# Hybrid attention block: softmax shares taken on the probabilities in place, next query's transposes moved, gate sums and last output block regrouped

## The chip, the cores and the metric

One core of a Trainium2 chip runs the whole program. The time is device microseconds of one execution. The kernel before was timed in three runs; the profile is of a further, single execution. Engines are named as in the profile: PE (TensorE, products), PEld (its weight loads), DVE (VectorE), ACT (ScalarE), POOL (GpSimd), SP (SyncE, which issues nearly all transfers).

## The reference

One layer of a diffusion backbone over 512 latent tokens and 256 context tokens, width 2048, float32. Both streams are normalised and modulated, and projected by one matrix `w_in`. Eight heads of a gated DeltaNet and eight heads of grouped-query attention follow; their gated outputs are concatenated and projected by `w_out`, and the residual sum is normalised:

```python
def attend(q_blk, k_all, v_all):
    s = jnp.einsum('bqkgd,bskd->bkgqs', q_blk, k_all).astype(jnp.float32) * (HEAD_DIM ** -0.5)
    p = jax.nn.softmax(s, axis=-1).astype(v_all.dtype)
    return jnp.einsum('bkgqs,bskd->bqkgd', p, v_all)

attn_lat = block_attention(qa, k_all, v_all) * jax.nn.silu(z_a)
y = jnp.concatenate([gdn_lat, attn_lat], axis=-1) @ w_out
x = x + gate * y                 # gate = (silu(c) @ w_ada + b_ada), last third
return rms_norm(x, final_norm_w)
```

Queries are 512 latent tokens by 8 heads of 128; keys and values are 768 tokens by 2 heads.

## The kernel before, in words

Large products are taken as three float32r products (`mm3`, L145 to L148): high by high, high by low and low by high part, where the high part is a cast on ACT and the low part a subtraction on DVE. Transposes and a few small products stay float32.

The program runs in stages: modulation and first projections (to 160 us), DeltaNet heads with the remaining projections as filler (to 876 us), attention with gate projections as filler (876 to 1114 us), the output projection in four column blocks of 512 (to 1293 us), and the last normalisation and store.

**Attention** is a loop over 17 steps, written at the end of the program's listing below. Step `u` works on half a head, 256 queries (a unit). On PE a unit has, in this order: transposes of the previous unit's probabilities (`pt`, two of three groups), the scores of this unit (`s`, 12 products), the third `pt` group, the spread of the previous unit's reciprocals (`ov`), filler steps, the values of the previous unit (`o`, 18 products of 256 columns), one filler step, the transposes of a query (`qtp`), two filler steps. A head's second unit transposes the next head's rotated query (`qn`) into `qTh` and `qTl`; a head's first unit transposes the raw query of the next head back to tokens for its norm.

PE, ACT, DVE and POOL run this stage in the order in which the code emits it; SP's order is set by a scheduler. So a DVE instruction that waits holds all behind it.

On ACT and DVE a unit has: the high and low parts of the transposed probabilities (`pth`, `ptl`), the row maximum of the scores (`mx`, L1260), two exponentials (`pr`, L1270) that also give the row sums, in second units the rotation of the next query (L1238 to L1241), two gate rows, filler work, two more gate rows, the result, the high and low parts of the next query. `attn_over` (L1275) then takes the reciprocals of the row sums and puts them on the diagonals of `dg`. One unit later `attn_spread` (L1296) multiplies ones by `dg` on PE, so that each reciprocal stands in a column for all partitions, and ACT copies the result to `ov`. `attn_values` (L1304) multiplies the values by `ov`; for ten units whose gate is there already it first multiplies the gate by `ov`.

PSUM buffers: `pt`, `ov` and `qtp` share two banks in turn (tag "t"); `s` has three, `o` one, filler `zl` two.

**Fillers.** `fillers` (L1344) projects 11 gate blocks (`zl`), 16 row tiles each in four weight pieces. A step is one row tile, three products. `z_piece` (L1338) loads a piece, two pieces ahead, and both casts it (`whi_z`) and subtracts (`wlo_z`). `z_over` closes a block: a Tanh on ACT, then `ze` and `M` on DVE. A unit runs FS, FV, FQ, FR = 4, 3, 1, 2 steps at the four places.

**Gate rows.** `gate_rows` (L1378) computes the output gate, a vector of 2048: 64 tiles of `w_ada` (`graw`) are multiplied by a column of `scol` and added into `gacc`, 16 tiles for each 512 columns. `gate_out` (L1369) sums `gacc` over partitions by a product with ones (`gater`), adds a row of `b_ada` and writes 512 values to memory (`grd`), four times in all. The rows are read back spread over all partitions (`gbc`) for the output stage.

**Last output block** (L1550 on): for each of four row tiles `t`, 48 products of 512 columns, `epilogue` (L1522: times gate, plus residual, square with row sum, times the norm's weights), the reciprocal root (`power`, on POOL), scaling of 2048 columns half on ACT and half on DVE, two transfers of 512 KB.

Of the kernel before, what the change touches and what calls it, by code (L numbers as in the profile page):

```python
# [8 lines left out]
F32 = mybir.dt.float32  # L9
F32R = mybir.dt.float32r  # L10
AF = mybir.ActivationFunctionType
# [57 lines left out]
def build(tc, a):  # L69
# [169 lines left out]
    def mul(eng, out, x, y):  # L239
        eng.tensor_tensor(out=out, in0=x, in1=y, op=ALU.mult)  # L240
# [970 lines left out]
    def ttile(shape, nm):  # L1211
        return PSt.tile(shape, F32, tag="t", bufs=2, name=nm)
# [3 lines left out]
    def attn_q(h):  # L1216
        qc = ap_.tile([128, SEQ], F32, tag="qc", bufs=2, name=f"qc{h}")
        SY.dma_start(qc, qad[h])
        return qc
# [52 lines left out]
            prs.append(pr)  # L1272
        return prs

    def attn_over(h, qp, mx):  # L1275

        dg = ap_.tile([128, 2, 128], F32, tag="dg", bufs=2, name=f"dg{h}_{qp}")
        V.reciprocal(mx[:, 1], mx[:, 1])
        V.tensor_tensor(out=dg, in0=ident.unsqueeze(1).to_broadcast([128, 2, 128]),
                        in1=mx[:, 1].unsqueeze(2).to_broadcast([128, 2, 128]), op=ALU.mult)  # L1280
        return dg

    def attn_pt(h, qp, prs, j2):

# [8 lines left out]
        split_from(tp3, pth, ptl)  # L1293
        return pth, ptl

    def attn_spread(h, qp, dg):  # L1296

        ov = ttile([128, 256], f"ov{h}_{qp}")
        T.matmul(ov, lhsT=ones, rhs=dg.rearrange("p a b -> p (a b)"), start=True, stop=True)
        over = ap_.tile([128, 256], F32, tag="ov", bufs=2, name=f"ov{h}_{qp}")  # L1300
        S.copy(over, ov)
        return over

    def attn_values(h, qp, pts, over):  # L1304
# [12 lines left out]

    done, early = set(), set()
# [19 lines left out]
    def z_piece(n):  # L1338
        i, kq = zs[n // 4], n % 4
        col = (COL_ZG if i < 8 else COL_ZA - 1024) + i * 128  # L1340
        src = w_in[kq * 512:(kq + 1) * 512, col:col + 128].rearrange("(k p) c -> p k c", p=128)
        return wpiece(src, f"z{i}_{kq}", 128, V)

    def fillers():  # L1344

        pieces = [z_piece(0), z_piece(1)]
        over = None
        yield
        for n in range(4 * len(zs)):
            i, kq = zs[n // 4], n % 4  # L1350
            if n + 2 < 4 * len(zs):
                pieces.append(z_piece(n + 2))
            if kq == 2 and outs:
                gate_out(*outs.pop(0))
            hi, lo = pieces.pop(0)
            if kq == 0:
                pl = PP.tile([128, SEQ], F32, tag="pl", name=f"zl{i}")
            for k4 in range(4):
                k = kq * 4 + k4
                for m, (lw, rt) in enumerate(((hi[:, k4], hhL[:, k]), (hi[:, k4], hl(0, k)), (lo[:, k4], hhL[:, k]))):  # L1360
                    T.matmul(pl, lhsT=lw, rhs=rt, start=k == 0 and m == 0, stop=k == KT - 1 and m == 2,  # L1361
                             skip_group_check=True)
# [6 lines left out]
    def gate_out(c, acc, row):  # L1369

        pr = PP.tile([128, 512], F32, tag="pl", name=f"gater{c}")
        T.matmul(pr[0:32], lhsT=ones[:, 0:32], rhs=acc, start=True, stop=True)
        V.tensor_tensor(out=row, in0=row, in1=pr[0:1], op=ALU.add)
        SY.dma_start(grd[:, c * 512:c * 512 + 512], row)

    outs = []

    def gate_rows():  # L1378

        def load(i):  # L1380
            c, k = divmod(i, KT)
            raw = ap_.tile([128, 512], F32, tag="graw", bufs=GB, name=f"graw{i}")
            SY.dma_start(raw, w_ada[k * 128:(k + 1) * 128, 2 * D + c * 512:2 * D + c * 512 + 512])
            return raw

        def bias(c):
            row = ap_.tile([128, 512], F32, tag="ze", bufs=2, name=f"grow{c}")[0:1]
            SY.dma_start(row, a["b_ada"][:, 2 * D + c * 512:2 * D + c * 512 + 512])
            return row

        raws = [load(i) for i in range(GB - 1)]
        acc = last = None
        yield
        for i in range(4 * KT):
            c, k = divmod(i, KT)
            raw = raws.pop(0)
            if k == 0:
                last, acc = acc, ap_.tile([128, 512], F32, tag="gacc", bufs=2, name=f"gacc{c}")
            if k == 0:
                V.tensor_scalar(out=acc, in0=raw, scalar1=scol[:, k:k + 1], scalar2=None, op0=ALU.mult)  # L1400
            else:
                V.scalar_tensor_tensor(out=acc, in0=raw, scalar=scol[:, k:k + 1], in1=acc, op0=ALU.mult, op1=ALU.add)  # L1402
            if i + GB - 1 < 4 * KT:
                raws.append(load(i + GB - 1))
            if k == 3 and c:
                outs.append((c - 1, last, bias(c - 1)))
            yield
        outs.append((3, acc, bias(3)))

    qcs = {i: attn_q(i) for i in (1, 2)}  # L1410
    for i in range(8):
# [21 lines left out]
    for u in range(2 * NH + 1):  # L1433
        h, qp = divmod(u, 2)
        more = h + 1 < NH
        prs, pts = None, []
        if before is not None:
            pts = [attn_pt(before[0], before[1], before[2], j2) for j2 in range(2)]
        if h < NH:
            sos, mx = attn_scores(h, qp, *qt, scs[h])  # L1440
        if before is not None:
            pts.append(attn_pt(before[0], before[1], before[2], 2))
            over = attn_spread(before[0], before[1], dg)
        if h < NH:
            prs = attn_exp(h, qp, sos, mx, scs[h])
            if qp == 1 and more:
                qn = next(qns)
            fill(FS + 5 * (before is None), 2)
        if before is not None:
            fill(FV, 2)  # L1450
            attn_values(before[0], before[1], pts, over)
        if u < NZA:

            e = ap_.tile([128, SEQ], F32, tag="ze", bufs=2, name=f"zae{u}")
            S.activation(e, M[8 + u], AF.Tanh, scale=0.5)
            silu(V, M[8 + u], M[8 + u], e)
            early.update(((u, 0), (u, 1)))
        fill(FQ)
        if more:
            if qp == 0:  # L1460
                qns = attn_norm(h + 1, qcs.pop(h + 1))
                next(qns)
                if h + 3 < NH:
                    qcs[h + 3] = attn_q(h + 3)
            else:
                qt = attn_qt(h + 1, qn)
        if h < NH:
            dg = attn_over(h, qp, mx)
        fill(FR)
        before = h, qp, prs  # L1470
    for _ in gen:
# [1 line left out]
    for _ in rows:  # L1473
        pass
    for o_ in outs:
        gate_out(*o_)
    es_m4.close()
    es_p0.close()
    es_p.close()
# [52 lines left out]
    for c in range(4):  # L1532
# [16 lines left out]
            wlast.append((hi, lo))  # L1549
        for t in range(4):  # L1550
            ts_ = slice(t * 128, t * 128 + 128)
            ps = PO.tile([128, 512], F32, tag="po", name=f"po3_{t}")
            for k in range(KT):
                mm3(ps, mh[k][:, ts_], ml[k][:, ts_], *wlast[k], k == 0, k == KT - 1)
            epilogue(c, t, ps)
            f = fr[:, t:t + 1]
            V.tensor_reduce(out=f, in_=fss[:, t], axis=AX.X, op=ALU.add)
            V.tensor_scalar(out=f, in0=f, scalar1=1.0 / D, scalar2=EPS, op0=ALU.mult, op1=ALU.add)
            power(f, -0.5)
            for q in range(2):  # L1560
                qs = slice(q * 1024, q * 1024 + 1024)
                if q == 0:
                    S.activation(yx[:, t, qs], yx[:, t, qs], AF.Copy, scale=f)
                else:
                    V.tensor_scalar(out=yx[:, t, qs], in0=yx[:, t, qs], scalar1=f, scalar2=None, op0=ALU.mult)
                SY.dma_start(a["out"][0, t * 128:t * 128 + 128, qs], yx[:, t, qs])
# [26 lines left out]
```

## Time and profile before

| what | value |
|---|---|
| median of 3 runs | 1307.14 us (1307.06 to 1307.84) |
| profiled execution, its own time | 1304.42 us |
| its span in the profile | 1302.6 us |
| PE, DVE, ACT, POOL busy | 1250.4, 842.5, 583.4, 141.9 us |
| attention, 876 to 1114 us | PE busy 232.84, DVE 187.25, ACT 116.52 of 238 us |
| output projection, 1114 to 1293 us | PE busy 178.9 of 179 us |
| after the last product, 1293 to 1302.6 us | PE 0, DVE 2.99, ACT 1.87 us |

In the profile a row of the timeline is: start, duration (both us, summed where `xN` merges instructions), engine, line, operation, tiles written and read, shape, and in brackets the idle time of the engine before it and what ended that. A line's name is that of the helper that emits it: L240 is the helper for a product of two tensors, L950 and L951 the split into high and low part, L1361 a filler's products. Matmul rows overlap, so the pace of PE is read from starts, not from durations.

### The profile page before, as it was taken

What the parts mean: (1) busy time and instruction counts of PE and PEld (TensorE: products, weight loads), DVE (VectorE), ACT (ScalarE), POOL (GpSimd) and SP (SyncE); (2) the same over time, 40 slices, a digit from 0 to 9 for tenths busy, and PEclk for the clock granted to TensorE, in tenths of its full rate; (3) what the DMA queues carried; (4) which work ended last, traced back from release to release, by engine and by line L of the source; (5) the groups of instructions that cost most, each with busy time, mean ns of one, the idle gap of its engine ahead of it and who ended that gap; (6) DMA issues with size and microseconds to landing.
All of it is one profiled execution on the core that took longest, in us unless ns stands there. A gap on an engine that the chain in (4) does not pass through costs nothing. (4 is left out here: it accounts for less than half of the span.)

```text
span 1302.6 us, 24348 instructions
## 1 busy us (share of the span) xinstructions
PE 1250.4 (96%) x9226; PEld 1018.4 (78%) x9226; DVE 842.5 (65%) x1893; ACT 583.4 (45%) x1464; POOL 141.9 (11%) x206
## 2 busy tenths in 40 slices
PE   6799999999999999999999999999999999999997
PEld 4466688888888888888888877787888888788885
DVE  5444596686867678675776646537888887555432
ACT  4222363455545454544545444535555444434211
POOL 1323100111111111111111001100000000000000
PEclk9999999999999999999999999999999999999998
DMA  9999424231332313222132443356443443475302
GB/s 354 316 326 347 133 67 107 60 67 55 74 72 62 78 47 83 67 69 57 54 83 75 106 131 110 99 164 214 149 129 114 123 140 102 161 244 190 93 33 97
DMA packets 227000, 164.53 MB, mean 126 GB/s; under 512 B 62210, under 2 KB 198491, under 8 KB 225859
## 3 DMA queue, kind: packets, MB, share of 16 engines
q1 hardware_dynamic: 226586, 162.87, 42.9%
q8 instruction: 73, 1.20, 0.4%
q14 instruction: 44, 0.36, 0.1%
q10 hardware_dynamic: 297, 0.11, 0.0%
HBM read 148.85 MB, written 14.08 MB: 125 GB/s over the span
## 5 line engine op out<-in xcount | busy, mean ns | idle before, releaser
L240 POOL TENSOR_TENSOR sdh<-sth,egl 128x256 f32<-128x256 f32 x80 | 56.9, 711 | 446.6 <-DVE sth L892 344.8
L871 ACT ACTIVATE oqh<-ksh,egsw 64x128 f32<-64x128 f32 x128 | 46.3, 362 | 92.7 <-DVE rh L866 86.4
L866 DVE SCALAR_TENSOR_TENSOR rh<-ksh,negeg,vtokh 64x128 f32<-64x128 f32 x176 | 61.2, 348 | 31.1 <-PE ksh L854 24.5
L146 PE MATMUL po<-whi_wo,mh 128*128 128x512 f32 x192 | 76.2, 397 | 0.0
L148 PE MATMUL po<-whi_wo,ml 128*128 128x512 f32 x192 | 76.1, 396 | 0.0
L147 PE MATMUL po<-wlo_wo,mh 128*128 128x512 f32 x192 | 76.1, 396 | 0.0
L1361 PE MATMUL zl<-hhL,whi_z 128*128 128x512 f32 x176 | 74.0, 421 | 0.0
L1361 PE MATMUL zl<-hhL,wlo_z 128*128 128x512 f32 x176 | 69.8, 396 | 0.0
L1361 PE MATMUL zl<-hL,whi_z 128*128 128x512 f32 x176 | 69.6, 395 | 0.0
L130 DVE TENSOR_TENSOR wlo_wo<-wraw_wo,whi_wo 128x512 fp32r<-128x512 f32 x48 | 33.0, 690 | 55.5 <-ACT whi_wo L129 55.3
L886 PE MATMUL tsh<-vsh,ktok 128*128 128x128 f32 x352 | 56.6, 283 | 6.7 <-ACT vnh L882 3.5
L886 PEld LDWEIGHTS tsh<-vsh,ktok 128*128 128x128 f32 x352 | 47.4, 190 | 16.0 <-ACT vnh L882 7.9
L129 ACT CAST whi_wo<-wraw_wo 128x512 fp32r<-128x512 f32 x48 | 29.6, 620 | 67.3 <-PE po L148 56.8
L892 DVE TENSOR_TENSOR sth<-sdh,tsh 128x256 f32<-128x256 f32 x80 | 33.6, 420 | 27.4 <-PE tsh L886 19.2
L879 ACT ACTIVATE vsh<-tsh,cch 128x128 f32<-128x128 f32 x88 | 32.2, 366 | 38.4 <-PE tsh L875 37.1
L164 PE MATMUL vl<-hhL,wlo_v 128*128 128x512 f32 x112 | 46.3, 413 | 0.0
L164 PE MATMUL vl<-hhL,whi_v 128*128 128x512 f32 x112 | 46.2, 413 | 0.0
L164 PE MATMUL vl<-hL,whi_v 128*128 128x512 f32 x112 | 45.8, 409 | 0.0
L1402 DVE SCALAR_TENSOR_TENSOR gacc<-graw,scol,gacc 128x512 f32<-128x512 f32 x60 | 44.9, 748 | 1.0
L950 ACT CAST pth<-pt 128x512 fp32r<-128x512 f32 x48 | 26.8, 585 | 40.7 <-PE pt L1289 40.7
L146 PEld LDWEIGHTS po<-whi_wo,mh 128*128 128x128 f32 x192 | 36.2, 188 | 9.5 <-ACT whi_wo L129 0.8
L148 PEld LDWEIGHTS po<-whi_wo,ml 128*128 128x128 f32 x192 | 36.2, 189 | 8.7
(540 smaller groups left out, 3890.2 us busy)
## 6 DMA issues: line engine op xcount, KB each, us to landing
wada<-in_w_ada SPq DMA_DIRECT2D x64, 512.0 KB, 8.6
graw<-in_w_ada SPq DMA_DIRECT2D x64, 256.0 KB, 3.1
wraw_wo<-in_w_out SPq DMA_DIRECT2D x48, 256.0 KB, 3.3
wraw_z<-in_w_in SPq DMA_DIRECT2D x44, 256.0 KB, 3.1
wraw_v<-in_w_in SPq DMA_DIRECT2D x28, 256.0 KB, 2.9
wraw_k<-in_w_in SPq DMA_DIRECT2D x24, 256.0 KB, 2.9
wraw_q<-in_w_in SPq DMA_DIRECT2D x24, 256.0 KB, 2.8
xs<-in_x SPq DMA_DIRECT2D x4, 1024.0 KB, 5.4
```

The source lines that it names most:

```text
L130: (lo_eng or G).tensor_tensor(out=lo, in0=raw, in1=hi, op=ALU.subtract)
L146: T.matmul(out, lhsT=lh, rhs=rh, start=start, stop=False, skip_group_check=True)
L147: T.matmul(out, lhsT=lh, rhs=rl, start=False, stop=False, skip_group_check=True)
L148: T.matmul(out, lhsT=ll, rhs=rh, start=False, stop=stop, skip_group_check=True)
L164: T.matmul(out, lhsT=lw, rhs=rt[m], start=k == 0 and n == 0, stop=k == KT - 1 and n == 2, skip_group_check=True)
L240: eng.tensor_tensor(out=out, in0=x, in1=y, op=ALU.mult)
L866: V.scalar_tensor_tensor(out=r[rows], in0=ks[rows, d], scalar=gsc["negeg"][rows, gcol:gcol + 1], in1=vtok[rows, p], op0=ALU.mult, op1=ALU.add)
L871: S.activation(oq[rows, v, p - 2], ks[rows, d], AF.Copy, scale=gsc["egsw"][rows, gcol:gcol + 1])
L886: T.matmul(ts[:, d], lhsT=ktok[:, p, half], rhs=vs, start=True, stop=True, skip_group_check=True)
L892: V.tensor_tensor(out=sn, in0=sd, in1=ts[:, 0:2], op=ALU.add)
L1361: T.matmul(pl, lhsT=lw, rhs=rt, start=k == 0 and m == 0, stop=k == KT - 1 and m == 2, skip_group_check=True)
L1402: V.scalar_tensor_tensor(out=acc, in0=raw, scalar=scol[:, k:k + 1], in1=acc, op0=ALU.mult, op1=ALU.add)
```

## The change

Five edits:

1. **Shares in place.** `attn_over` and `attn_spread` go. `attn_share` takes the reciprocals and multiplies both tiles of probabilities (128 queries by 768 keys) by their column of reciprocals, in place, on DVE, in the same unit. `attn_values` then needs no `ov`: one DVE instruction instead of two for the ten units with an early gate, a copy instead of a product for the other six.
2. **Next query's transposes** (`attn_qt`) stand ahead of the values instead of behind them.
3. **Gate rows** two of four per unit move from ahead of the values to behind them, and the low part of a filler's weight piece (`z_low`) is emitted two steps after its cast.
4. **Gate sums at once.** Each block of 512 keeps its own `gacc`; the row of `b_ada` is added to partition 0 of it, and at the end of the stage four products, each on its own 32 columns of PE, sum all four; one copy, one transfer.
5. **Last row tile of the last output block** in two halves of 256 columns with steps of their own, and its 2048 columns scaled and stored in four parts of 512 instead of two of 1024.

```diff
-    def attn_over(h, qp, mx):
-        dg = ap_.tile([128, 2, 128], F32, tag="dg", bufs=2, name=f"dg{h}_{qp}")
+    def attn_share(prs, mx):
         V.reciprocal(mx[:, 1], mx[:, 1])
-        V.tensor_tensor(out=dg, in0=ident.unsqueeze(1).to_broadcast([128, 2, 128]),
-                        in1=mx[:, 1].unsqueeze(2).to_broadcast([128, 2, 128]), op=ALU.mult)
-        return dg
+        for qi, pr in enumerate(prs):
+            V.tensor_scalar(out=pr, in0=pr, scalar1=mx[:, 1, qi:qi + 1], scalar2=None, op0=ALU.mult)
...
-    def attn_spread(h, qp, dg):
-        ov = ttile([128, 256], f"ov{h}_{qp}")
-        T.matmul(ov, lhsT=ones, rhs=dg.rearrange("p a b -> p (a b)"), start=True, stop=True)
...
         if (h, qp) in early:
-            V.scalar_tensor_tensor(out=m, in0=m, scalar=0.5, in1=over, op0=ALU.mult, op1=ALU.mult)
-            mul(V, m, op, m)
+            V.scalar_tensor_tensor(out=m, in0=m, scalar=0.5, in1=op, op0=ALU.mult, op1=ALU.mult)
         else:
-            mul(V, m, op, over)
+            V.tensor_copy(m, op)
...
+    def z_low(raw, hi, lo):
+        V.tensor_tensor(out=lo, in0=raw, in1=hi, op=ALU.subtract)
...
+                if k4 == 2 and n + 2 < 4 * len(zs):
+                    z_low(*pieces[-1])
                 yield
...
+    def gate_bias(acc, row):
+        V.tensor_tensor(out=acc[0:1], in0=acc[0:1], in1=row, op=ALU.add)
+
+    def gate_out(accs):
+        pr = PP.tile([128, 512], F32, tag="pl", name="gater")
+        for c, acc in enumerate(accs):
+            T.matmul(pr[32 * c:32 * c + 32], lhsT=ones[:, 0:32], rhs=acc, start=True, stop=True, skip_group_check=True)
+        row = ap_.tile([128, 512], F32, tag="ze", bufs=2, name="grow")
+        S.copy(row, pr)
+        SY.dma_start(grd.rearrange("o (c n) -> (o c) n", c=4), row[0:128:32])
...
         if before is not None:
-            fill(FV, 2)
-            attn_values(before[0], before[1], pts, over)
+            fill(FV)
+        if more and qp == 1:
+            qt = attn_qt(h + 1, qn)
+        if h < NH:
+            attn_share(prs, mx)
+        if before is not None:
+            attn_values(before[0], before[1], pts)
...
-        fill(FQ)
+        fill(FQ, 2)
...
+                for q in range(2):
+                    hs = slice(q * 256, q * 256 + 256)
+                    ws = slice(c * 512 + q * 256, c * 512 + q * 256 + 256)
+                    ps = PO.tile([128, 256], F32, tag="po", name=f"po3_{t}_{q}")
+                    for k in range(KT):
+                        hi, lo = [w[:, hs] for w in wlast[k]]
+                        mm3(ps, mh[k][:, ts_], ml[k][:, ts_], hi, lo, k == 0, k == KT - 1)
+                    tt = op_.tile([128, 512], F32, tag="tt", bufs=2, name=f"tt{c}_{t}_{q}")
+                    y = yx[:, t, ws]
+                    mul(V, tt[:, 0:256], ps, gbc[:, ws])
+                    V.tensor_tensor(out=tt[:, 0:256], in0=y, in1=tt[:, 0:256], op=ALU.add)
+                    S.activation(tt[:, 256:512], tt[:, 0:256], AF.Square, accum_out=fl[:, q:q + 1])
+                    mul(V, y, tt[:, 0:256], fwb[:, ws])
...
+            n = 1024 if t < 3 else 512
+            for q in range(D // n):
```

How the order changes on DVE, in the second unit of head 4, from the gate weights ahead of the values to the first low part of the next unit (`wlo_z` and `ze`, `M` are filler work, `gacc` gate rows, `M<-o` the result, `mx` the reciprocals, `pr` the probabilities). Before:

```order
L1402 SCALAR_TENSOR_TENSOR gacc_11352<-graw_11354,scol,gacc_11352 128x512
L130 TENSOR_TENSOR wlo_z_2_11505<-wraw_z_2_11502,whi_z_2_11504 128x512
L1402 SCALAR_TENSOR_TENSOR gacc_11352<-graw_11360,scol,gacc_11352 128x512
L237 SCALAR_TENSOR_TENSOR ze_11518<-ze_11518,zl_11263 128x512
L1326 SCALAR_TENSOR_TENSOR M_10036<-ze_11518,M_10036 128x512
L1402 SCALAR_TENSOR_TENSOR gacc_11352<-graw_11486,scol,gacc_11352 128x512
L1312 SCALAR_TENSOR_TENSOR M_10043<-M_10043,ov_0_11466 128x256
L240 TENSOR_TENSOR M_10043<-o_0_11528,M_10043 128x256
L951 TENSOR_TENSOR qTl_11558<-qtp_11552,qTh_11557 128x512
L1278 RECIPROCAL mx_1_11452<-mx_1_11452 128x2
L1279 TENSOR_TENSOR dg_1_11561<-cmain,mx_1_11452 128x256
L130 TENSOR_TENSOR wlo_z_3_11567<-wraw_z_3_11564,whi_z_3_11566 128x512
```

Now the same stretch on DVE, in the changed kernel:

```order
L1337 TENSOR_TENSOR wlo_z_1_11439<-wraw_z_1_11437,whi_z_1_11438 128x512
L237 SCALAR_TENSOR_TENSOR ze_11473<-ze_11473,zl_11230 128x512
L1315 SCALAR_TENSOR_TENSOR M_10036<-ze_11473,M_10036 128x512
L1337 TENSOR_TENSOR wlo_z_2_11463<-wraw_z_2_11461,whi_z_2_11462 128x512
L951 TENSOR_TENSOR qTl_11487<-qtp_11481,qTh_11486 128x512
L1277 RECIPROCAL mx_1_11417<-mx_1_11417 128x2
L1279 TENSOR_SCALAR pr_1_0_11429<-pr_1_0_11429,mx_1_11417 128x768
L1279 TENSOR_SCALAR pr_1_1_11431<-pr_1_1_11431,mx_1_11417 128x768
L1302 SCALAR_TENSOR_TENSOR M_10043<-M_10043,o_0_11493 128x256
L1406 SCALAR_TENSOR_TENSOR gacc_11292<-graw_11358,scol,gacc_11292 128x512
L1406 SCALAR_TENSOR_TENSOR gacc_11292<-graw_11446,scol,gacc_11292 128x512
L951 TENSOR_TENSOR ptl_1_0_11539<-pt_1_0_11533,pth_1_0_11538 128x512
```

The low part of the next query and the two scalings stand ahead of the result now, and two gate rows behind it; the scalings are what the next unit's transposes on PE read.

On PE, in the same unit of head 4, the place of the next query's transposes (`qtp`) among the last value product (`o`) and the filler steps (`zl`), before:

```order
L148 MATMUL o_0_11528<-pth_0_2_11460,val 128x256
L1361 MATMUL zl_11508<-hhL,whi_z_0_11364 128x512
L1361 MATMUL zl_11508<-hL_600,whi_z_0_11364 128x512
L1361 MATMUL zl_11508<-hhL,wlo_z_0_11365 128x512
L955 MATMUL qtp_11552<-cmain,qn_11400 128x128 x4
L1361 MATMUL zl_11508<-hhL,whi_z_1_11478 128x512
```

On PE in the changed kernel, the same transposes, with the first value products behind them:

```order
L1358 MATMUL zl_11466<-hhL,whi_z_0_11321 128x512
L1358 MATMUL zl_11466<-hL_600,whi_z_0_11321 128x512
L1358 MATMUL zl_11466<-hhL,wlo_z_0_11322 128x512
L955 MATMUL qtp_11481<-cmain,qn_11367 128x128 x4
L146 MATMUL o_0_11493<-pth_0_0_11391,vah 128x256
L147 MATMUL o_0_11493<-ptl_0_0_11392,vah 128x256
```

Between these transposes and the next unit's first `pt` stand 18 value products and three filler steps, where two filler steps stood.

More of the change, by code (lines that the diff above doesn't have):

```diff
@@ L1294, in attn_pt, with attn_values @@
         return pth, ptl
-    def attn_spread(h, qp, dg):
-        ov = ttile([128, 256], f"ov{h}_{qp}")
[L1299 to L1304, printed above, removed]
+    def attn_values(h, qp, pts):
         kv = h // 4
@@ L1340, in z_piece @@
         col = (COL_ZG if i < 8 else COL_ZA - 1024) + i * 128
-        src = w_in[kq * 512:(kq + 1) * 512, col:col + 128].rearrange("(k p) c -> p k c", p=128)
-        return wpiece(src, f"z{i}_{kq}", 128, V)
+        raw, hi, lo = [wp.tile([128, 4, 128], t_, tag=j, bufs=3, name=f"{j}_z{i}_{kq}")
+                       for j, t_ in (("wraw", F32), ("whi", F32R), ("wlo", F32R))]
+        SY.dma_start(raw, w_in[kq * 512:(kq + 1) * 512, col:col + 128].rearrange("(k p) c -> p k c", p=128))
+        S.copy(hi, raw)
+        return raw, hi, lo
+    def z_low(raw, hi, lo):
+        V.tensor_tensor(out=lo, in0=raw, in1=hi, op=ALU.subtract)
     def fillers():
         pieces = [z_piece(0), z_piece(1)]
+        for x in pieces:
+            z_low(*x)
         over = None
@@ L1353, in fillers @@
             if kq == 2 and outs:
-                gate_out(*outs.pop(0))
-            hi, lo = pieces.pop(0)
+                gate_bias(*outs.pop(0))
+            _, hi, lo = pieces.pop(0)
             if kq == 0:
@@ L1367, in fillers @@
         z_over(*over)
[L1369 to L1376, printed above, removed]
+    def gate_bias(acc, row):
[7 more added lines that the diff above has]
+        SY.dma_start(grd.rearrange("o (c n) -> (o c) n", c=4), row[0:128:32])
+    outs, accs = [], []
     def gate_rows():
@@ L1391, in gate_rows @@
         raws = [load(i) for i in range(GB - 1)]
-        acc = last = None
         yield
@@ L1397, in gate_rows @@
             if k == 0:
-                last, acc = acc, ap_.tile([128, 512], F32, tag="gacc", bufs=2, name=f"gacc{c}")
+                acc = ap_.tile([128, 512], F32, name=f"gacc{c}")
+                accs.append(acc)
             if k == 0:
@@ L1405, in gate_rows @@
             if k == 3 and c:
-                outs.append((c - 1, last, bias(c - 1)))
+                outs.append((accs[c - 1], bias(c - 1)))
             yield
-        outs.append((3, acc, bias(3)))
+        outs.append((acc, bias(3)))
     qcs = {i: attn_q(i) for i in (1, 2)}
@@ L1442, in build @@
             pts.append(attn_pt(before[0], before[1], before[2], 2))
-            over = attn_spread(before[0], before[1], dg)
         if h < NH:
@@ L1457, in build @@
             early.update(((u, 0), (u, 1)))
-        fill(FQ)
[L1459 to L1468, printed above, removed]
+        fill(FQ, 2)
+        if more and qp == 0:
+            qns = attn_norm(h + 1, qcs.pop(h + 1))
+            next(qns)
+            if h + 3 < NH:
+                qcs[h + 3] = attn_q(h + 3)
         fill(FR)
@@ L1475, in build @@
     for o_ in outs:
-        gate_out(*o_)
+        gate_bias(*o_)
+    gate_out(accs)
     es_m4.close()
@@ L1559, in build @@
             power(f, -0.5)
-            for q in range(2):
-                qs = slice(q * 1024, q * 1024 + 1024)
-                if q == 0:
+            n = 1024 if t < 3 else 512
+            for q in range(D // n):
+                qs = slice(q * n, q * n + n)
+                if q % 2 == 0:
                     S.activation(yx[:, t, qs], yx[:, t, qs], AF.Copy, scale=f)
```

20 lines of the change are left out of this document (14 added, 6 removed).

## Prediction

> **What bounds the kernel now.** I read the page's first lines, then busy time by stretch, then who TensorE waits for in the attention stretch, then the order of events in one unit and after the last product.
>
> ```profile
> span 1302.6 us, 24348 instructions
> PE 1250.4 (96%) x9226; PEld 1018.4 (78%) x9226; DVE 842.5 (65%) x1893; ACT 583.4 (45%) x1464; POOL 141.9 (11%) x206
> ```
>
> TensorE (PE) is busy for 96% of the span, so what shortens its own work shortens the program, unless another engine then makes it wait. By stretch, with each engine's busy time (and instructions):
>
> ```profile
> core 0: us, PE busy (x) PEld busy (x) DVE busy (x) ACT busy (x) POOL busy (x), PEclk, DMA share, GB/s
> 876.00:1114.00 238.00, 232.84 (x1299) 194.57 (x1297) 187.25 (x311) 116.52 (x261) 8.49 (x7) 1.00 0.45 138
> 1249.00:1293.00 44.00, 43.90 (x193) 35.84 (x191) 14.96 (x29) 8.42 (x17) 1.67 (x3) 1.00 0.18 72
> 1293.00:1302.60 9.60, 0.00 (x0) 0.00 (x0) 2.99 (x6) 1.87 (x3) 0.55 (x1) 0.61 0.27 109
> ```
>
> The first row is attention, 16 units (half a head, 256 queries) of about 14 us. PE is idle there for 238.0 - 232.84 = 5.2 us; VectorE (DVE) has 238 - 187 = 51 us free, at full clock. So PE's work is the bound and DVE is second. The last row is the tail: 9.6 us in which PE does nothing. PE's waits in attention (us, times, longest):
>
> ```profile
> PE pt L1289 <- DVE qTl L951: 3.0, 3, 1.2
> PE pt L1289 <- DVE ptl L951: 1.7, 2, 1.4
> ```
>
> Both are transposes of probabilities that wait for DVE to empty a PSUM buffer.
>
> **The change part by part.** *Removed from PE: the spread of the reciprocals (ov), 16 times, and three of four gate products (gater).* Starts around both:
>
> ```profile
> 1018.51 0.60 PE L1299 MATMUL ov<-dg,cmain 128*128 128x256 f32 x2
> ...
> 1019.18 0.41 PE L1361 MATMUL zl<-hL,whi_z 128*128 128x512 f32 x1
> 1019.42 0.39 PE L1361 MATMUL zl<-hhL,wlo_z 128*128 128x512 f32 x1
> ...
> 1020.12 0.39 PE L1361 MATMUL zl<-hhL,wlo_z 128*128 128x512 f32 x1
> 1020.43 1.04 PE L1372 MATMUL gater<-gacc,cmain 128*32 128x512 f32 x2
> ...
> 1021.74 0.40 PE L1361 MATMUL zl<-hL,whi_z 128*128 128x512 f32 x1
> ```
>
> Gate-projection products (zl) follow each other every (1020.12 - 1019.18) / 4 = 0.235 us. From ov's start to the second zl after it are 0.67 us; less one zl that is 0.44 us for ov. Around the gate product lie 1021.74 - 1020.12 = 1.62 us, less two zl 1.15 us. Nothing hides either, PE being the bound: 16 x 0.44 = 7.0 us, 3 x 1.15 = 3.4 us. The fourth gate product becomes four, each on its own 32 columns, at the same place. An earlier stretch shows such a pattern, 16 instructions that are eight products on four column groups:
>
> ```profile
> 44.90 1.92 PE L355 MATMUL ada<-wada,cs 128*32 128x512 f32 x16
> ```
>
> Four take 0.96 us, as one gater does now, so the end pays no more; if they went singly, it would be 3 us more.
>
> *Added on DVE: 32 scalings, 128x768, in place.* No row has the size; these have the operation (ns min/median/max):
>
> ```profile
> L1400 DVE TENSOR_SCALAR gacc<-graw,scol x4: 480/481/482, 884.0 to 1051.9; 128x512 f32<-128x512 f32 x4
> L1565 DVE TENSOR_SCALAR yx<-yx,fr x4: 754/754/756, 1264.1 to 1296.8; 128x1024 f32<-128x1024 f32 x4
> L1279 DVE TENSOR_TENSOR dg<-cmain,mx x16: 421/425/450, 890.2 to 1097.0; 128x256 f32<-128x256 f32 x16
> L240 DVE TENSOR_TENSOR M<-o,M x10: 423/425/425, 902.2 to 1027.4; 128x256 f32<-128x256 f32 x10
> ```
>
> Halfway between 481 and 754 is 618 ns; the second row is in place as well. I take 0.62 us. The upper bound is the pace of the two-input rows below (0.69 us for 512, 0.42 for 256, so 0.96 for 768). DVE gains 32 x 0.62 = 19.8 us and loses dg (16 x 0.43 = 6.8) and ten of the products with the result (4.2): +8.8 us against 51 free. ACT loses 16 copies of ov and bounds nothing. What matters is where they stand. [...]
>
> *The new wait.* The next unit's first transposes (pt) now need both scalings, which stand in DVE's queue behind the unit's other work. I replay the fullest kind of unit, the second half of a head, from the present trace of one that also closes a gate block (ze, M):
>
> ```profile
> 1000.80 1.04 PE L1289 MATMUL pt<-cmain,pr 128*128 128x128 f32 x8
> 1006.95 0.98 ACT L1270 ACTIVATE pr<-s,mx,hss 128x768 f32<-128x768 f32 x1
> 1008.56 0.69 DVE L130 TENSOR_TENSOR wlo_z<-wraw_z,whi_z 128x512 fp32r<-128x512 f32 x1
> 1009.17 1.53 DVE L1402 SCALAR_TENSOR_TENSOR gacc<-graw,scol,gacc 128x512 f32<-128x512 f32 x2
> 1010.62 0.68 DVE L130 TENSOR_TENSOR wlo_z<-wraw_z,whi_z 128x512 fp32r<-128x512 f32 x1
> ...
> 1011.88 0.68 DVE L237 SCALAR_TENSOR_TENSOR ze<-ze,zl 128x512 f32<-128x512 f32 x1
> 1012.60 0.69 DVE L1326 SCALAR_TENSOR_TENSOR M<-ze,M 128x512 f32<-128x512 f32 x1
> 1013.21 0.74 DVE L1402 SCALAR_TENSOR_TENSOR gacc<-graw,scol,gacc 128x512 f32<-128x512 f32 x1
> 1014.25 0.60 PE L1289 MATMUL pt<-cmain,pr 128*128 128x128 f32 x4
> 1015.34 0.16 DVE L1278 RECIPROCAL mx<-mx 128x2 f32<-128x2 f32 x1
> 1015.47 0.66 PE L1289 MATMUL pt<-cmain,pr 128*128 128x128 f32 x4 [0.62 <-DVE qTl L951]
> ```
>
> The unit's PE work runs from 1000.80 to 1014.25, 13.45 us; without ov the next pt is due at 1013.81. In the new order DVE does, from 1008.56: two gate rows 1.45, one wlo 0.61, ze and M 1.33, another wlo 0.61, qTl 0.60, the reciprocal 0.19, the scalings 0.53 and 0.62. That ends at 1014.50: a wait of about 0.7 us. The exponentials end near 1008, so they are not last. Without ze and M the scalings end at 1013.17, 0.6 us in time. The order has four such units with a closing gate block ahead of the scalings (heads 0, 1, 4, 5) and two with a 0.6 us bias row there (heads 2, 6), which break even; head 3 has neither, head 7 no rotation. So the new waits are 4 x 0.7 = 2.8 us. First halves of heads have no rotation and no qTl ahead of the scalings, 2.7 us less on DVE, and never wait. Behind a waiting pt stand all of PE's products, so each such wait is paid in full.
>
> *The old wait that goes.* In the last row above pt is held for qTl, by 1015.47 - 1014.25 - 0.44 = 0.8 us. The transposes of the next query now stand ahead of 18 value products, so qTl is done before pt asks: the 3.0 us of that wait go. Ahead of the values the transposes need the rotated query. The rotation ends as the wlo at 1008.56 starts, and without ov they would be due where the values start now (the row at 1009.54 below) less 0.44, at 1009.1. That is 0.5 us of cover; a DVE later than that stops PE there, with the values behind.
>
> Two gate rows per unit move behind the values, with the loads that they set free on SP's queue, where the gate weights' loads stand behind them:
>
> ```profile
> graw<-in_w_ada SPq DMA_DIRECT2D x64, 256.0 KB, 3.1
> ```
>
> A load lands in 3.1 us and is issued three rows, at least half a unit or 6 us, ahead: nothing, and if that cover is gone DVE waits and the scalings with it. The low part of a gate weight piece comes two filler steps (1.4 us) later than its cast, still six steps (4 us) before its use: nothing.
>
> I take old and new waits as a draw: 0. Bounds: all 5.2 us of idle go (-5.2), or each scaling takes 0.96 us and the second halves come 0.7 us later: 4 x 0.7 + 2 x 0.7 + 0.1 = +4.3.
>
> *The tail.* The last block's last row tile is cut in two halves of 256 columns, and its output in four transfers.
>
> ```profile
> 1009.54 0.28 PE L146 MATMUL o<-pth,vah 128*128 128x256 f32 x1
> ...
> 1011.58 0.29 PE L148 MATMUL o<-pth,val 128*128 128x256 f32 x1
> 1281.80 0.39 PE L146 MATMUL po<-wlh,mh 128*128 128x512 f32 x1
> ...
> 1292.51 0.39 PE L148 MATMUL po<-wlh,ml 128*128 128x512 f32 x1
> 1292.93 0.69 DVE L240 TENSOR_TENSOR tt<-po,gbc 128x512 f32<-128x512 f32 x1 [6.31 <-PE po L148]
> 1296.81 1.15 ACT L1563 ACTIVATE yx<-yx,fr 128x1024 f32<-128x1024 f32 x1 [1.64 <-POOL fr L234]
> L1566 SPq DMA_DIRECT2D out_y<-yx x8: 332/362/420, 1264.9 to 1298.0; - x8
> DMA to landing us min/median/max: 2.6/2.7/2.7
> ```
>
> The 256-column products go every 2.04 / 17 = 0.12 us, the 512-column ones every 10.71 / 47 = 0.228. So 96 x 0.12 against 48 x 0.228: +0.6, less 0.1 for the shorter last one. The chain behind now takes 1296.81 + 1.15 - 1292.93 = 5.0 us to the first transfer. With 256 columns: product and sum 0.5 each, square with its sum 0.55, one small step 0.25, power 0.6, a 512-column scaling 0.6: 3.0 us. Its product with the norm weights no longer waits for the square and lies beside it; the first half's steps lie beside the second half's 48 products (5.8 us). SP needs 0.36 us per transfer: the last is issued 3 x 0.36 later, at 4.1, before at 5.4: -1.3. Tail: -0.8 (from -1.5, if the first transfer decides, to +0.8, if four small ones land later than two). [...]
>
> Sum: -7.0 - 3.4 + 0 - 0.8 = -11.2 us. The profiled execution took 1304.42 us (span 1302.6 and 1.8 around it) and becomes 1293.2; the median of the runs, 1307.14, lies 2.7 above and I shift it alike: 1296.
>
> **The rivals.** *DVE late everywhere.* The scalings run at 0.96 us or DVE starts each unit late: +4.3, so 1300. For it: DVE has 187 + 9 = 196 us of work in a stretch that shrinks to 228, in fixed order. Against: both TENSOR_SCALAR rows.
> *The waits vanish:* -5.2 instead of 0, 1291. For it: all their releasers are moved. Against: the replay.
> *Slower: the scalings become the bound.* Place: the scalings of the second halves. If DVE reaches them x us later than replayed, PE waits 4 (0.7 + x) + 2 x + (x - 0.6) = 7 x + 2.2 us in heads 0 to 6. At x = 2.5 that is 19.7, of which 2.8 is counted: 19.7 - 2.8 - 11.2 = +5.7, 1313. It takes the whole gain at x = 1.7. For it: DVE is in order, and a late load or cast ahead of the scalings holds them. Against: the casts and loads of the replayed unit held nothing.
> *It does not do what it says:* the four gate products go singly, +3, 1299.
>
> **How the numbers follow.** A measurement of this kernel tells about 0.2%, 2.6 us, from no change. Forecast (-8.5 to -13.5): 0.56. DVE late or gate products single (-2.6 to -8.5): 0.22. Waits vanish (beyond -13.5): 0.09. Within 0.2%: 0.07. Slower: 0.06. So faster 0.87. The range leaves out the far end of the waits that vanish and what lies above 1302, some 0.18 in all: 1292 to 1302.
>
> **What would show it.** Right: ov gone, attention about 228 us, TENSOR_SCALAR pr at 0.62 us, PE waiting for pr under 4 us and no more for qTl, four gater products within 1.2 us, the chain behind the last product 2 us shorter. Wrong: scalings near 0.96, PE waiting for pr in most units, or a tail not shorter than 9.6 us.

## The result, and the profile after

The changed kernel takes 1293.13 us (median of four runs, 1291.58 to 1293.93), the kernel before 1307.18 in the same comparison: ratio 0.989, 95% interval 0.9873 to 0.9907, 14 us less. The profiled execution took 1292.93 us, with a span of 1291.1. First the stretches: start of the program to the first score product, from there to the first output product (attention), from there to the last output product, tail. Columns: length, busy time (and instructions) of each engine, granted clock, transfers. Before:

```profile
core 0: us, PE busy (x) PEld busy (x) DVE busy (x) ACT busy (x) POOL busy (x), PEclk, DMA share, GB/s
0.00:876.41 876.41, 839.08 (x7163) 679.65 (x7163) 569.23 (x1443) 407.06 (x1091) 131.16 (x195) 0.99 0.43 121
876.41:1114.25 237.84, 232.68 (x1298) 194.33 (x1296) 187.50 (x311) 116.77 (x262) 8.49 (x7) 1.00 0.45 137
1114.25:1292.90 178.65, 178.65 (x768) 144.44 (x768) 82.76 (x134) 57.74 (x109) 1.67 (x3) 1.00 0.42 140
1292.90:1302.60 9.70, 0.00 (x0) 0.00 (x0) 3.05 (x6) 1.87 (x3) 0.55 (x1) 0.61 0.27 108
```

and after:

```profile
0.00:877.96 877.96, 840.11 (x7162) 680.86 (x7163) 568.77 (x1443) 407.77 (x1091) 131.18 (x195) 0.99 0.43 120
877.96:1103.00 225.04, 222.35 (x1266) 187.24 (x1264) 194.63 (x318) 111.98 (x246) 9.27 (x7) 1.00 0.49 145
1103.00:1282.40 179.40, 179.30 (x820) 147.05 (x816) 83.70 (x140) 59.13 (x112) 1.66 (x3) 1.00 0.42 140
1282.40:1291.10 8.70, 0.00 (x0) 0.00 (x0) 2.25 (x6) 1.84 (x4) 0.55 (x1) 0.68 0.33 121
```

Row by row: +1.55, -12.80, +0.75, -1.00, together -11.5. The medians differ by 14, because the profiled execution before was 2.8 us faster than its median (1304.42 against 1307.18). The first row is code that the change does not touch. Attention gives it all: TensorE's busy time falls by 10.3 us, its idle time from 5.16 to 2.69. VectorE gets 7.1 us more in a shorter stretch and still has 30 free.

TensorE's waits there in the kernel after (us, times, longest):

```profile
PE pt L1287 <- DVE ptl L951: 1.4, 2, 1.0
PE pt L1287 <- DVE pr L1279: 0.9, 1, 0.9
PE pt L1287 <- ACT qn L1230: 0.2, 1, 0.2
```

No wait for qTl is left, and one for pr. The scalings, from the view of the tile pr (ns min/median/max, first and last start):

```profile
L1279 DVE TENSOR_SCALAR pr<-pr,mx x32: 611/616/622, 886.4 to 1084.5; 128x768 f32<-128x768 f32 x32
```

They take what the prediction took, 0.62 us. From the timeline, the unit that the prediction replayed, head 4's second half, starting here at 996.28, and the gate products:

```profile
996.28 1.03 PE L1287 MATMUL pt<-cmain,pr 128*128 128x128 f32 x8
...
1007.96 0.69 DVE L951 TENSOR_TENSOR qTl<-qtp,qTh 128x512 fp32r<-128x512 f32 x1
1008.56 0.16 DVE L1277 RECIPROCAL mx<-mx 128x2 f32<-128x2 f32 x1
1008.75 1.15 DVE L1279 TENSOR_SCALAR pr<-pr,mx 128x768 f32<-128x768 f32 x2
1009.52 1.31 PE L1287 MATMUL pt<-cmain,pr 128*128 128x128 f32 x8
...
1101.99 1.06 PE L1375 MATMUL gater<-gacc,cmain 128*32 128x512 f32 x8
1102.99 0.50 PE L146 MATMUL po<-whi_wo,mh 128*128 128x512 f32 x1
```

The second scaling ends at 1009.90, 13.62 us into the unit (replay: 13.70). The transposes, due 13.01 us in (the length of a unit that waits for nothing, 944.14 to 957.15), start 0.23 late, when the first scaling (1008.75 + 0.62) is done, and take 1.31 us instead of 1.03 because the third of them waits for the second. The last rows are the four gate products: 1.00 us to the next product.

The tail after, from the timeline: the chain behind the last product, then SyncE's issues:

```profile
1282.02 0.28 PE L148 MATMUL po<-wlh,ml 128*128 128x256 f32 x1
1282.34 0.42 DVE L240 TENSOR_TENSOR tt<-po,gbc 128x256 f32<-128x256 f32 x1 [3.89 <-PE po L148]
...
1284.10 0.55 POOL L234 TENSOR_TENSOR fr<-fr,expo 128x1 f32<-128x1 f32 x1 [9.43 <-DVE fr L1583]
1284.68 1.33 ACT L1589 ACTIVATE yx<-yx,fr 128x512 f32<-128x512 f32 x2 [0.85 <-POOL fr L234]
1284.68 0.88 DVE L1591 TENSOR_SCALAR yx<-yx,fr 128x512 f32<-128x512 f32 x2 [0.66 <-POOL fr L234]
1285.20 0.33 SPq L1592 DMA_DIRECT2D out_y<-yx  x1
...
1286.42 0.33 SPq L1592 DMA_DIRECT2D out_y<-yx  x1
1286.86 0.39 SPq L1592 DMA_DIRECT2D out_y<-yx  x1
```

The power ends 2.3 us behind the start of VectorE's first operation (1282.34) instead of 3.8. But the third transfer waits for ScalarE's second scaling, and the last is issued 4.5 us behind that start (before 5.1). The landing is on record for the first two of the four, 2.1 and 2.4 us after their issue. Before, it is on record for the first transfer of each earlier row tile alone (2.6 to 2.7). From the first issue to the end of the span pass 5.9 us (before 5.0).

### The profile page after: what moved, and what is told of

The parts are those of the page before. It is cut to its first block, busy times and chain, and to the rows that moved or that the text cites. A ratio compares the mean times of both kernels' runs of the same rounds, so it can differ in the third digit from the quotient of the medians.

```text
span 1291.1 us, 24373 instructions
## 1 busy us (share of the span) xinstructions
PE 1241.8 (96%) x9242; PEld 1015.1 (79%) x9242; DVE 849.4 (66%) x1905; ACT 580.7 (45%) x1452; POOL 142.7 (11%) x206
## 5 line engine op out<-in xcount | busy, mean ns | idle before, releaser
L1358 PE MATMUL zl<-hhL,whi_z 128*128 128x512 f32 x176 | 71.4, 405 | 0.0
```

## The experiments

Two theories. *Place*: VectorE does its work in order, and what counts is how late the scalings of a head's second half end after the transposes are due. *Share*: VectorE has 30 us free, and small moves are absorbed. Attention is measured as above, from each run's profile; "idle" is its length less TensorE's busy time. The length of a unit is taken from its first score product to the first of the next unit; where nothing waits it is 13.45 us before and 13.01 after. Times are ratios to the kernel before on the same chip, with 95% interval.

| kernel | attention us | idle | clock | time ratio |
|---|---|---|---|---|
| before | 237.8 | 5.2 | 1.00 | 1 |
| after | 225.0 | 2.7 | 1.00 | 0.989 (0.9873-0.9907) |
| order_old | 272.5 | 28.7 | 0.92 | 1.0259 (1.0233-1.0285) |
| gates_early | 234.9 | 9.7 | 0.99 | 0.9979 (0.9968-0.9990) |
| qt_late | 235.5 | 12.3 | 1.00 | 0.9988 (0.9977-0.9999) |
| share_first | 224.9 | 3.3 | 1.00 | 0.9911 (0.9894-0.9929) |
| order_new | 237.5 | 4.6 | 1.00 | 1.0008 (0.9999-1.0018) |
| gates_once | 234.3 | 4.9 | 1.00 | 0.9979 (0.9968-0.9990) |
| spread_kept | 230.7 | 1.7 | 1.00 | 0.9937 (0.9924-0.9950) |
| scale_twice | 233.1 | 9.1 | 1.00 | 0.9962 (0.9947-0.9977) |
| scale_thrice | 254.1 | 19.9 | 0.96 | 1.0112 (1.0096-1.0128) |
| share_act | 234.0 | 10.2 | 0.99 | 0.9973 (0.9964-0.9983) |
| last_only | 237.3 | 4.9 | 1.00 | 0.9988 (0.9977-1.0000) |

**order_old**: the changed kernel with the old order.

```diff
-            fill(FV)
-        if more and qp == 1:
-            qt = attn_qt(h + 1, qn)
-        if h < NH:
-            attn_share(prs, mx)
+            fill(FV, 2)
...
-        fill(FQ, 2)
+        fill(FQ)
...
+        if more and qp == 1:
+            qt = attn_qt(h + 1, qn)
+        if h < NH:
+            attn_share(prs, mx)
         fill(FR)
```

> The scaling in place stays, but the order of the kernel before comes back: two gate rows ahead of the values, the next query's transposes behind them, and the scalings last, where the reciprocals were spread. Place theory (VectorE works in order, and what counts is how late the scalings of a head's second half end after the transposes are due): from the trace of the changed kernel, VectorE reaches the second scaling of such a unit about 1.9 us later than now (two gate rows 1.45, the product with the values' result 0.42), 4 x 1.9 in heads 0, 1, 4, 5, 2 x 1.8 in heads 2 and 6, 1.5 in head 3: +12.7 us, about 1306, with TensorE waiting for pr some 13 us. Share theory (VectorE is busy for 195 of 225 us, so 30 us are free and moves of 1 to 2 us are absorbed): no change, 1293.

Measured: attention 47.5 us longer, 2.6% over the kernel before. The share theory falls, and my size was far too small. Its stretch, in the columns above:

```profile
879.50:1152.00 272.50, 243.84 (x1263) 202.21 (x1261) 196.60 (x317) 112.77 (x246) 8.27 (x7) 0.92 0.40 120
```

TensorE's waits there:

```profile
PE pt L1287 <- DVE pr L1279: 27.3, 15, 3.4
```

It waits for pr 15 times. Two places of the timeline, the end of a first half and score products after a wait:

```profile
928.43 0.17 DVE L1233 TENSOR_SCALAR hss<-hss 128x4 f32<-128x4 f32 x1 [2.47 <-ACT hjk L1232]
928.50 0.16 DVE L1277 RECIPROCAL mx<-mx 128x2 f32<-128x2 f32 x1
928.70 1.15 DVE L1279 TENSOR_SCALAR pr<-pr,mx 128x768 f32<-128x768 f32 x2
929.47 1.32 PE L1287 MATMUL pt<-cmain,pr 128*128 128x128 f32 x8 [2.03 <-DVE pr L1279]
...
950.01 0.63 PE L146 MATMUL s<-kTh,qTh 128*128 128x512 f32 x1
950.44 0.63 PE L147 MATMUL s<-kTl,qTh 128*128 128x512 f32 x1
950.87 0.63 PE L148 MATMUL s<-kTh,qTl 128*128 128x512 f32 x1
```

Two things were missed. In first halves the next query's norm (hss) stands ahead of the scalings and holds VectorE for ScalarE, 2.5 us in the rows above and 15.1 us in seven waits, so all units but one wait, not seven. And after a long wait TensorE runs slower: the last rows, behind a wait of 2.15 us, follow each other every 0.43 us, where 512-column products otherwise take 0.235; the granted clock there (947.69 to 951.29) is 0.56. Idle time rises by 26.0 us, busy time of nearly the same work by 21.5.

**gates_early**: two gate rows ahead of the values again.

```diff
-            fill(FV)
+            fill(FV, 2)
...
-        fill(FQ, 2)
+        fill(FQ)
```

> Only the two gate rows of a unit go back ahead of the values, so 1.45 us of VectorE's work stand ahead of the scalings again. Place theory: second halves of heads pay it less their slack in the trace of the changed kernel (none in heads 0, 1, 4, 5; 0.1 in heads 2 and 6; 0.7 in head 3): 4 x 1.45 + 2 x 1.35 + 0.75 = +9.2 us, about 1302; first halves, 2 to 3 us in time, pay nothing. Share theory: no change, 1293.

Measured +9.9 us of attention, ratio 0.9979: the place theory holds to a microsecond. The seven second halves are 8.8 us longer together (9.2 expected). Another 1.0 us the theory did not have: after the longest wait, 2.05 us in head 0, the next unit's 12 score products took 3.17 us instead of 1.96. TensorE's waits:

```profile
PE pt L1287 <- DVE pr L1279: 8.0, 7, 2.0
PE pt L1287 <- DVE ptl L951: 1.4, 2, 1.0
```

Seven waits, the seven second halves with a head to follow: 1.45 us of VectorE's work moved ahead of the scalings takes away 9.9 of the 12.8 us.

**qt_late**: the transposes behind the values. The gate rows follow them, in the last filler steps of the unit.

```diff
-        if more and qp == 1:
-            qt = attn_qt(h + 1, qn)
...
-        fill(FQ, 2)
+        fill(FQ)
...
-        fill(FR)
+        if more and qp == 1:
+            qt = attn_qt(h + 1, qn)
+        fill(FR, 2)
```

> Only the next query's transposes go back behind the values, ahead of the gate rows. Place theory: qTl no longer stands ahead of the scalings, so TensorE's waits for pr (0.9 us, and 0.3 in the four transposes' pace three times) go, -1.9; but the waits for qTl of the kernel before come back, 3.0 us in three places: +1.1, about 1294, within what a measurement tells. If the transposes' move did nothing for TensorE: no wait for qTl and 1291.

TensorE's waits:

```profile
PE pt L1287 <- DVE ptl L951: 8.9, 9, 1.8
PE pt L1287 <- DVE qTl L951: 3.1, 4, 1.1
PE pt L1287 <- DVE pr L1279: 0.2, 1, 0.2
```

The two waits came out as expected (qTl 3.1, pr 0.2), the time did not, by 9 us: the rows, now some 1.4 us later, stand right ahead of the next unit's ptl, and nine units wait 0.3 to 1.8 us for that. So the run does not price the transposes' move by itself. Of the three places tried, the gate rows are free in one alone: behind the values, with filler steps after them.

**share_first**: the two statements ahead of the values in the other order, scalings first.

```diff
-        if more and qp == 1:
-            qt = attn_qt(h + 1, qn)
         if h < NH:
             attn_share(prs, mx)
+        if more and qp == 1:
+            qt = attn_qt(h + 1, qn)
```

> The scalings are issued ahead of the next query's transposes, so qTl (0.6 us on VectorE) stands behind them instead of ahead. Place theory: the scalings of heads 0, 1, 4, 5 end 0.6 us earlier, in time, and qTl, needed 0.87 us after the first transposes of the probabilities, is in time too: the waits for pr, some 1.9 us, go: about 1291. Rival: qTl becomes what TensorE waits for, or the waits for pr have another releaser: 1293.

The waits for pr are gone, and attention is as long (224.9). TensorE's waits:

```profile
PE pt L1287 <- DVE ptl L951: 2.3, 4, 1.0
PE pt L1287 <- ACT qn L1230: 0.7, 1, 0.7
PE pt L1287 <- DVE qTl L951: 0.2, 1, 0.2
```

What pr gave came back at ptl, qn and qTl, above all in head 0. My -1.9 was wrong.

**order_new**: the kernel before with the moves of the order alone; the low parts of the filler's weights stay right behind their casts.

```diff
-            fill(FV, 2)
+            fill(FV)
+        if more and qp == 1:
+            qt = attn_qt(h + 1, qn)
+        if before is not None:
             attn_values(before[0], before[1], pts, over)
...
-        fill(FQ)
+        fill(FQ, 2)
...
-            else:
-                qt = attn_qt(h + 1, qn)
```

> The kernel before with only the moves of the order: the next query's transposes ahead of the values, two gate rows behind them. The spread of the reciprocals, the four single gate products and the last block stay. If the moves free TensorE of its waits for qTl by themselves: attention 237.8 -> about 234.8 us, 3.0 less, waits for ptl (1.7) as before: ratio 0.9977. If the moves only protect the scalings and are worth nothing without them (two gate rows then lie ahead of the reciprocals and the third part of the probabilities): no change.

TensorE's waits:

```profile
PE pt L1289 <- DVE ptl L951: 4.3, 4, 2.0
PE pt L1289 <- ACT qn L1230: 0.4, 1, 0.4
```

and VectorE and TensorE around one of the waits for ptl, behind two gate rows:

```profile
908.62 0.15 DVE L1278 RECIPROCAL mx<-mx 128x2 f32<-128x2 f32 x1
908.81 0.42 DVE L1279 TENSOR_TENSOR dg<-cmain,mx 128x256 f32<-128x256 f32 x1
909.16 0.68 DVE L130 TENSOR_TENSOR wlo_z<-wraw_z,whi_z 128x512 fp32r<-128x512 f32 x1
909.76 1.28 DVE L951 TENSOR_TENSOR ptl<-pt,pth 128x512 fp32r<-128x512 f32 x2
...
910.50 0.66 PE L1289 MATMUL pt<-cmain,pr 128*128 128x128 f32 x4 [1.47 <-DVE ptl L951]
```

No change: the 3.0 us for qTl go, and 2.6 come back at ptl. The moves gain nothing alone; the scalings without them cost 2.6%; together they belong to the 1.1% that is gained.

**gates_once**: the kernel before with the gate sums joined as in the change.

```diff
-                gate_out(*outs.pop(0))
+                gate_bias(*outs.pop(0))
...
-        gate_out(*o_)
+        gate_bias(*o_)
+    gate_out(accs)
```

> The kernel before with only the gate rows' sums joined: four products on four column groups at the end instead of four at four times. By the prediction's second term: 3 x 1.15 = -3.4 us, ratio to before 0.9974, the four products within 1.1 us. If the single products lay in time that TensorE had to wait anyway: no change.

Measured -3.5 us of attention, ratio 0.9979: the term of the prediction.

**spread_kept**: the changed kernel with the spread's product back on TensorE, result unused.

```diff
             pts.append(attn_pt(before[0], before[1], before[2], 2))
+            ov = ttile([128, 256], f"ov{before[0]}_{before[1]}")
+            T.matmul(ov, lhsT=ones, rhs=cmain[:, 0:256], start=True, stop=True)
+            over = ap_.tile([128, 256], F32, tag="ov", bufs=2, name=f"ov{before[0]}_{before[1]}")
+            S.copy(over, ov)
```

> The changed kernel with the spread's product left in (on data that lies there from the start, its result copied and not used): TensorE gets the 16 products back and nothing waits for them. By the prediction's first term 16 x 0.44 = +7.0 us against the changed kernel, ratio to before 0.994 to 0.995. The product lies between the third transposes and the gate projection, ahead of the scalings in time, so part of it is given back where the scalings are late by 0.2 to 1 us (heads 0, 1, 4, 5: up to 4 x 0.4): +5.4 to +7.0. If the gain came from the waits, +2 or less.

Attention +5.7 us, busy time +6.6 (228.97 against 222.35), idle time -1.0: the product costs 16 x 0.41 us, and part of it fills the waits for pr.

**scale_twice** and **scale_thrice**:

```diff
             V.tensor_scalar(out=pr, in0=pr, scalar1=mx[:, 1, qi:qi + 1], scalar2=None, op0=ALU.mult)
+        for pr in prs * 1:
+            V.tensor_scalar(out=pr, in0=pr, scalar1=ones[:, 0:1], scalar2=None, op0=ALU.mult)
```

(`prs * 2` in the second.)

> The changed kernel with each pair of scalings followed by a second pair that multiplies by one: VectorE gets 32 more operations of 128x768, 1.07 us per pair at the pace of the first pair, all ahead of the transposes. Place theory: second halves of heads pay it less their slack: 4 x 1.07 (heads 0, 1, 4, 5) + 2 x 0.95 (2, 6) + 0.35 (3) = +6.5 us, in single waits of up to 1.3 us, and 2.0 us in head 0; first halves, 1 to 3 us in time, pay nothing: about 1300. Share theory (212 of 225 us busy): no change.

> The same with two more pairs, 2.14 us. Place theory with a constant price per microsecond: 4 x 2.14 + 2 x 2.05 + 1.4 + two units with about 1 us of slack 0.7 + 1.2: +16 us, 1309. Clock theory: after waits of 1.72 us and more in the kernel with the old order the 12 score products took 2.8 to 3.6 us instead of 1.96, after waits up to 1.39 us they did not; here six waits would be 2.0 to 3.0 us, so 6 x 1.2 = 7 us on top: +23, 1316, and the granted clock of the stretch falls below 0.98; in the kernel with two pairs only one wait (2.0 us, head 0) is that long, and the clock stays at 0.99.

The first lengthens attention by 8.1 us (6.5 expected), the second by 29.1, 21 more for the same step. Its stretch:

```profile
880.70:1134.80 254.10, 234.17 (x1266) 193.90 (x1264) 227.32 (x382) 112.34 (x246) 9.27 (x7) 0.96 0.43 129
```

Idle time grew by 17.2 us, which a constant price forecast (16); busy time grew by 11.8 at a clock of 0.96. The clock theory holds in kind: in four units the 12 score products took 2.7 to 3.6 us instead of 1.96. But 7 us was too little. VectorE is busy for 227 of 254 us, so its share of the stretch is still not the bound.

**share_act**: the scalings on ScalarE; the last row tile's output in two transfers.

```diff
-            V.tensor_scalar(out=pr, in0=pr, scalar1=mx[:, 1, qi:qi + 1], scalar2=None, op0=ALU.mult)
+            S.activation(pr, pr, AF.Copy, scale=mx[:, 1, qi:qi + 1])
...
             fill(FS + 5 * (before is None), 2)
+            attn_share(prs, mx)
...
-        if h < NH:
-            attn_share(prs, mx)
...
-            n = 1024 if t < 3 else 512
-            for q in range(D // n):
-                qs = slice(q * n, q * n + n)
+            cut = 1024 if t < 3 else 768
+            for q, qs in enumerate((slice(0, cut), slice(cut, D))):
```

> The changed kernel with the scalings moved to ScalarE, right behind the first four filler steps of a unit (there the reciprocals are taken too), and the last row tile's output in two transfers, of 768 columns scaled by ScalarE and 1280 by VectorE. Place theory: ScalarE, busy for 112 of 225 us, takes about 1 us per scaling and is done some 2 us before the transposes are due, so the waits for pr (1.9 us) go and those for ptl stay: attention 225.0 -> about 223 us. Tail: the last of two transfers is issued when VectorE's 1280 columns are done, 0.95 us after the power against 2.2 now, and lands in about 2.5 instead of 2.3: 8.7 -> 7.7 us. Together -3, about 1290 (ratio to before 0.987). Rival: ScalarE's casts of the weight pieces and its copies of the probabilities come 2 us later and TensorE waits for those: attention longer than 225.

The rival came true: attention 234.0 us. Its waits, TensorE's and then VectorE's longest:

```profile
PE pt L1287 <- DVE qTl L951: 6.6, 5, 2.1
PE pt L1287 <- DVE ptl L951: 3.3, 4, 1.8
...
DVE wlo_z L1337 <- ACT whi_z L1333: 14.3, 10, 2.4
```

ScalarE's casts of the weight pieces come behind its scalings, VectorE waits 14.3 us for them in order (2.8 in the changed kernel), and qTl behind them is late. In the tail the two transfers, the last issued at 1294.4, landed in 2.9 and 3.9 us instead of the 2.1 and 2.4 on record, which took back the earlier issue: 8.9 us from the last product's start, in the changed kernel 9.1.

**last_only**: the last block's edit put into the kernel before (the last part of the change's diff).

```diff
+                for q in range(2):
+                    hs = slice(q * 256, q * 256 + 256)
...
+            n = 1024 if t < 3 else 512
```

> The kernel before with only the last row tile in two halves and its output in four transfers. The prediction said -0.8 (from -1.5 to +0.8). By the two traces it is -0.25: the stretch of output products 0.75 us longer, the tail behind the last product 1.0 us shorter. Either is within what a measurement tells: ratio 0.998 to 1.001; the two stretches of its profile decide.

Ratio 0.9988; output products 179.0 us long (before 178.3, each to the start of the last one), tail 8.3 from there (10.1). The two give -1.1. In ten kernels with the new tail and the same four transfers it lies between 8.3 and 9.4; last_only has the 8.3, the other nine 8.7 and more.

**gates_same_cols**: the changed kernel with four more gate products.

```diff
+        for _ in range(4):
+            T.matmul(pr[0:32], lhsT=ones[:, 0:32], rhs=accs[0], start=True, stop=True, skip_group_check=True)
         row = ap_.tile([128, 512], F32, tag="ze", bufs=2, name="grow")
```

> The changed kernel with four more gate products behind the four, all on the same 32 columns (the first sum again, to the same place). If the four products are done within 1.06 us because each has its own column group, these four take 4 x 1.0 us: the output products start 4 us later after the gate products than now (1.0). If being issued back to back is what makes them cheap, 1 us later.

From its timeline, the four products, the four more, and the first output product:

```profile
1101.20 1.07 PE L1375 MATMUL gater<-gacc,cmain 128*32 128x512 f32 x8
1102.09 3.60 PE L1377 MATMUL gater<-gacc,cmain 128*32 128x512 f32 x8
1105.61 0.50 PE L146 MATMUL po<-whi_wo,mh 128*128 128x512 f32 x1
```

Four on four column groups take 0.89 us to the next start, four on the same columns 3.52. So the four are cheap because each has columns of its own, and not because they follow each other at once (one run, this profile).

## Why the prediction was right, and where it was not

The mechanism was right; the time, 1293.1 for 1296, lies inside the range, 3 us below the forecast. That the profiled execution fell by 11.5 us where 11.2 were worked out is in part luck: the waits gave 2.4 us more than forecast, the tail 0.55 less, and 1.55 were lost ahead of attention. By the medians the change is -14.05, beyond the -13.5 that the list of chances gives to waits that vanish. They did not vanish: 2.7 us of idle time are left, and the new waits in the transposes.

- *Spread off TensorE, -7.0*: right. A unit that waits for nothing is 0.44 us shorter, as worked out. Put back, the product costs 6.6 us of busy time and 5.7 of attention.
- *Three gate products, -3.4*: right. Joined alone they give -3.5, and the four take 1.00 us to the next product. The rival of single products (+3) falls with gates_same_cols.
- *Scalings at 0.62 us*: right, 0.616. VectorE gained 7.1 us, not 8.8, mostly because two in a row start 0.53 apart (16 x 0.09 = 1.4).
- *New and old waits a draw, 0*: the mis-sized term. Attention fell by 12.8 us, the removed products make 10.4 of it, and 2.4 are left for the waits. The second halves of heads 1, 4 and 5 were 1.45, 0.85 and 0.32 us longer than a unit that waits for nothing, and are 0.38, 0.50 and 0.39 longer now. So the old wait cost more than the list of waits shows (1.2, 0.6 and nothing for these three). The new one stands where the replay put it, in heads 0, 1, 4 and 5, but is smaller: the second scaling holds only the third transpose, so the replayed unit loses 0.23 + 0.28 = 0.5 us, not 0.7. Most of it shows as busy time, transposes of 1.3 instead of 1.03 us, and not in the list. In head 0 the listed wait is 0.95 us; 0.6 of it is a VectorE operation of the output block (ml), which stands between the reciprocal and the scalings. The new waits sum to about 2.5 us (0.95 + 0.28 in head 0, and the three above), where 2.8 were forecast.
- *Gate rows and low parts moved, at nothing*: no row waits for its load in the changed kernel, as forecast. But their place is not worth nothing: two rows back ahead of the values cost 9.9 us (gates_early), and rows at the end of the unit, with the transposes behind the values, 10.5 (qt_late).
- *Tail, -0.8*: measured -0.25 in this profile (+0.75 and -1.00), about -1.1 in last_only: within the bounds. The first transfer leaves 1.8 us earlier (2.0 worked out); the last only 0.6 (1.3 worked out), because ScalarE scales two quarters one after the other. The trace before tells the landing of the first of two transfers alone (2.6 to 2.7 us), so it does not price four small ones against two. From the first issue to the end of the span two took 5.0 us and four 5.9.
- *The shift of 2.7 us*: the step that failed in the last line. It took the profiled execution's distance to the median of before as lasting; after, profile (1292.93) and median (1293.13) agree. Where the profiled execution before gained its 2.7 us is not shown. Of the 1.55 us lost ahead of attention, too, the cause stays open; the clock between 20 and 40 us was 0.82, before 0.89.
- *Slower, if the scalings come x later*: its price, 7 x + 2.2, gives 9.7 us of waits at x = 1.07; less the 2.5 that the changed kernel pays already that is +7.2, measured +8.1. At 2.14 it gives +14.7 against 29.1: it is near the idle time (+17.2) and misses the clock.

The moves alone (-0.3), the gate sums (-3.5) and the spread (-5.7) make -9.5 of attention's -12.8. The other 3.3 us appear only in the whole change: with the moves, waits for ptl are 4.3 us without the scalings and 1.4 with them. Three things of the kernel before that hold VectorE ahead of ptl are gone from there in the changed kernel: the second product with the result (0.4 us), the reciprocals and dg behind the moved gate rows (0.5 by the starts in order_new's rows), and a low part (0.6). Which of them frees ptl was not tried and stays open.

No kernel here beats the changed one: share_first is not told from it, the rest are slower.

## What to carry to other kernels

When work goes from the bound engine to one with free time, ask where in that engine's order it lands and what it stands behind: here the same 32 operations belong to a gain of 1.1% in one order and to a loss of 2.6% in another, with VectorE busy for 194.6 and 196.6 us. Replay the fullest unit with the durations of the trace; here it gave the end of the scalings to 0.1 us (13.62 for 13.70). Take moves that gain nothing alone into account: they can be what makes another edit pay.

## What the runs showed of the hardware

Long waits of TensorE cost nearly twice: order_old has 26.0 us more idle time and 21.5 more busy time for nearly the same work, scale_thrice 17.2 and 11.8. After waits for pr of up to 1.39 us the 12 score products took their usual 1.96 us from first to last start; after waits of 1.62 to 2.06 us sometimes 1.95, mostly 2.8 to 3.3; after all longer ones 2.5 to 3.6. The granted clock behind two of these waits (order_old, 2.15 us; gates_early, 2.05 us) was 0.56 and 0.62, and 1.00 behind one of 2.05 us that cost nothing (scale_thrice, 941.20 to 943.60). What decides in the mixed cases no run shows.

ScalarE scales 128x768 in 0.93 us (share_act), VectorE in 0.62.
